# Two pooling groups per copy, pooling products later in the weave, and a weave paced by due times

## The chip, the cores and the metric

The kernel runs on one core of one Trainium2 chip. The metric is the device time of one execution in microseconds (us). Engines: PE is TensorE (matmul), DVE is VectorE, ACT is ScalarE, POOL is GpSimd, SP issues the weight transfers.

## The reference, cut to what matters

Two layers of a decoder trunk over 256 positions and 1024 channels, in float32. Each layer: half a SwiGLU, a mixer, half a SwiGLU, a gated embedding. The change lies in the mixer:

```
u = RMSNorm(h);  columns of u @ w_in go to three branches and their gates
A) sparse attention: indexer, top 64 keys of a query as a mask, softmax, values
B) pooling: for windows w = 2, 4, 8, 16, one group of 128 channels each:
       pooled = windowsum(x_g, w) / count - x_g ;  mixed = pooled @ w_pool[g] * scale
C) Mamba-2 SSD: conv, chunked scan in 2 chunks of 128, gated by silu(z), RMSNorm
h += W_out( sum_b sigmoid(gate_b) * Lift_b(branch_b) )
```

## The kernel before, in words

Everything is held with channels on partitions and the 256 positions in the free dimension. To keep float32 accuracy each operand is split into a high and a low part, and a product is three matmuls (`mm3`, L166 high-high, L167 low-high, L168 high-low). Weights stream in units of 128x1024: a DMA from SP into `raw`, a cast on ACT to `whi` (L140), a subtraction on DVE to `wlo` (L141). PSUM has two rings of four banks: `mm` for products with weights, `aux` for everything else.

In the mixer the work of the branches is written as Python generators, and `weave` takes steps from them in turn: always from the one whose share of steps done, `x[0] / x[3]`, is smallest. The number beside each generator is its count of steps. The scheduler of the tile framework then sets the order on each engine from its own estimate of times; instructions emitted with `keep` (and all in `mm`, L106, and `transpose`, L109) hold their order among themselves on PE.

There are two weaves a layer. The first has `choose` (indexer, top keys), `silus` (conv and gate inputs) and twelve steps of `gates`. The second has

- `states`: the SSD. Scans on DVE (L919), exponentials on ACT (L924), a product with the masked scores (L925), then `near` products on PE, added by L941; at the end of each half the carried state (L945, L952, L960, L962), the gate by silu(z) (L970), squares (L223, L225) and the split with the gain (L189, L190).
- `attend`: scores, `softmax` (L744 and L746 to L750), transposes of the probabilities (L109), copies (L761), values.
- `pools`: for two groups at a time the input projection into one bank of `mm`, then for each group `pool_group`: memset of a pad (L983), copy out of the bank (L984), one to four doubling adds (L988, L989), a correction (L993), the subtraction (L996), the split of the result (`split`, L185 and L186), and three matmuls with `w_pool`.
- `gate`: the rest of the gates' projections, plain `mm` work that fills PE.

`states` and `attend` are `apart`: when both have come to a step that yields a function, the functions are called one behind the other, so that the PE work with 64 rows or columns of both stands together. These are the common runs; there are four of them in a layer.

In `pool_group` a group's copy is emitted when its turn comes, so the second group's copy of a pair comes behind the first group's whole chain. The t1 buffers (six) hold the copy and all results of the chain. After the second weave come the lift products (in `mm` banks), the output projection and the next half.

Of the kernel before, what the change touches and what calls it, by code (L numbers as in the profile page):

```python
# [16 lines left out]
P = 128  # L17
D = 1024
S = 256
# [11 lines left out]

LINE = 128
WINDOWS = (2, 4, 8, 16)


CC = {}
# [28 lines left out]
class Builder:  # L65
    def __init__(self, ctx, tc, ins, out, order=None):
        self.tc = tc
        self.nc = tc.nc
        self.ins = ins
        self.out = out  # L70
        self.n = 0
        self.order, self.used, self.made = order, [], []
        self.todo = None
        self.gap = None

        def pool(name, bufs, **kw):
            return ctx.enter_context(tc.tile_pool(name=name, bufs=bufs, **kw))

        self.const = pool("const", 1)
        self.wp = pool("wp", 1)  # L80
        self.act = pool("act", 1)
        self.tmp = pool("tmp", 1)
        self.small = pool("small", 1)
        self.ps = pool("ps", 1, space=bass.MemoryType.PSUM)
        self.dram = pool("dram", 1, space=bass.MemoryType.DRAM)
# [328 lines left out]
    def in_steps(self, layer, i, u, ps):  # L414
        for j in range(2):
            w = self.unit(layer, U_IN + i + j, 1024)
            for k in range(KD):
                s = slice(k * P, (k + 1) * P)
                self.mm3(ps[:, j * S:(j + 1) * S], (w[0][:, s], w[1][:, s]),
                         (u[0][:, k], u[1][:, k]), k == 0, k == KD - 1)  # L420
                if k % 4 == 3:
                    yield

    def mix(self, layer, nxt):
# [63 lines left out]
        def choose():  # L488
            v4 = self.t([P, 4], tag="v4", bufs=1)
            nc.vector.tensor_scalar(v4[:, :2], ss[:, :2], 1.0 / 256, EPS, op0=OP.mult, op1=OP.add)  # L490
            nc.vector.tensor_scalar(v4[:, 2:], ss[:, 2:], 1.0 / 64, EPS, op0=OP.mult, op1=OP.add)
            rk = self.t([P, 4], tag="rk", bufs=1)
            self.rsqrt(rk, v4, 4)
            for h in range(2):
                nc.vector.tensor_scalar(cn[:, h], cn[:, h], rk[:, h:h + 1], None, op0=OP.mult)
                nc.vector.tensor_scalar(ki2[:, h], sm[:, h, None, 8:72].to_broadcast([P, 2, 64]),
                                        rk[:, 2 + h:3 + h], None, op0=OP.mult)
            yield
            yield
            yield  # L500
            pk = self.bank("aux")
            for h in range(2):
                self.transpose(pk[:, h * P:(h + 1) * P],
                                    ki2[:, h].rearrange("p a b -> p (a b)"), self.ident)
            self.split_scaled(ki[0], ki[1], pk[:, :S], self.col(layer, "idx_k_norm"))
            yield
            yield
            pc = self.bank("aux")
            for c in range(2):
                for h in range(2):  # L510
                    self.transpose(pc[:, c * S + h * P:c * S + (h + 1) * P],
                                        cn[:, h, c * P:(c + 1) * P], self.ident)
            for c in range(2):
                self.split_scaled(ct[:, 0, c], ct[:, 1, c], pc[:, c * S:(c + 1) * S],
                                  self.col(layer, "kv_norm", c))
            yield
            mb[0] = yield from self.indexer(layer, 0, sm, qi, ki, idx[:, 0])
            mb[1] = yield from self.indexer(layer, 1, sm, qi, ki, idx[:, 1])
# [32 lines left out]
        def some(n):  # L551
            for _ in range(n):
                next(gate)
                yield

        self.weave((choose(), 26), (silus(), 60), (some(12), 12))


        ya = self.a([P, 2, 4, S], FR, "a8", 2)
# [29 lines left out]
        def states():  # L589
            res["ssd"] = yield from self.ssd(layer, sm, xs, bc, cb, zs, big1[:, 16:22])  # L590

        def pools():
            wpl = self.unit(layer, U_POOL, 512)
            for i in range(0, 4, 2):
                ps = self.bank()
                yield from self.in_steps(layer, T_XP + i, u, ps)
                ps = ps.rearrange("p (a b) -> p a b", a=2)
                for j in range(2):
                    yield from self.pool_group(layer, i + j, ps[:, j], wpl, yp)

        with self.tc.issue_after(self.last.ins):
            self.weave((states(), 56), (attend(), 34), (pools(), 24), (gate, 43), apart=(0, 1))
        ysh, ysl, rs = res["ssd"]

        mh = self.a([P, 8, S], FR, "uh", 2)
# [39 lines left out]
    def weave(self, *gens, apart=()):  # L645

        left = [[0, i, g, n] for i, (g, n) in enumerate(gens)]  # L650
        apart, parked = set(apart), {}
        while left:
            x = min((x for x in left if x[1] not in parked), key=lambda x: (x[0] / x[3], x[1]))
            x[0] += 1
            call = next(x[2], x)
            if call is x:
                left.remove(x)
                apart.discard(x[1])
            elif call is not None:
                parked[x[1]] = call  # L660
            if parked and len(parked) == len(apart):
                for i in sorted(parked):
                    parked[i]()
                parked = {}

    def conv(self, layer, i, ps, xs, bc):
        nc = self.nc
# [63 lines left out]
    def softmax(self, h, two, mb, out):  # L731

        nc = self.nc
        nb = h + 1
        nk = nb * P
        per = 512 // nk
        prs = []
        for ps, _ in two:
            pr = self.t([P, per, nk])
            mx = self.t([P, per], tag="mx", bufs=2)  # L740
            sums = self.t([P, per], tag="sum", bufs=2)
            for j in range(per):
                x = mx[:, j:j + 1]
                nc.vector.tensor_tensor_reduce(pr[:, j], ps[:, j * nk:(j + 1) * nk], mb[:, :nk],  # L744
                                               1.0, 3.0e38, OP.add, OP.min, accum_out=x)
                self.last = nc.scalar.activation(pr[:, j], pr[:, j], AF.Exp, bias=x, scale=-1.0,  # L746
                                                 accum_out=sums[:, j:j + 1])
            nc.vector.reciprocal(sums, sums)
            for j in range(per):
                nc.scalar.mul(pr[:, j], pr[:, j], sums[:, j:j + 1])  # L750
            prs.append(pr)
            yield
        for _ in range(3):
            yield
        for (_, heads), pr in zip(two, prs):
            pt = self.bank("aux")
            for j in range(4):
                self.transpose(pt[:, j * P:(j + 1) * P],
                               pr[:, j // nb, (j % nb) * P:(j % nb + 1) * P], self.ident)
            th = self.t([P, 4, P])  # L760
            nc.scalar.copy(th, pt.rearrange("p (a b) -> p a b", a=4))  # L761
            out.append((heads, th))
            yield
# [211 lines left out]
        _, rs = self.rnorm(gap=2)  # L975
        return ysh, ysl, rs

    def pool_group(self, layer, g, ps, wpl, yp):
        nc = self.nc
        w = WINDOWS[g]  # L980
        pad = 16
        x = self.t([P, pad + S + 16], tag="t1")[:, :pad + S]
        nc.vector.memset(x[:, :pad], 0.0)  # L983
        nc.scalar.copy(x[:, pad:], ps)  # L984
        cur, have = x, 1
        while have < w:
            n = self.t([P, pad + S + 16], tag="t1")[:, :pad + S]
            nc.vector.tensor_copy(n[:, :have], cur[:, :have])  # L988
            nc.vector.tensor_tensor(n[:, have:], cur[:, have:], cur[:, :pad + S - have], op=OP.add)  # L989
            cur, have = n, 2 * have  # L990
        yield

        nc.vector.tensor_tensor(cur[:, pad:pad + 16], cur[:, pad:pad + 16],  # L993
                                self.col(layer, "pool_corr", g * 16, 16), op=OP.mult)
        y = self.t([P, S], tag="t1")
        nc.vector.scalar_tensor_tensor(y, cur[:, pad:], 1.0 / w, x[:, pad:],  # L996
                                       op0=OP.mult, op1=OP.subtract)
        yh = self.t([P, S], FR, tag="t1")
        yl = self.t([P, S], FR, tag="t1")
        self.split(yh, yl, y)  # L1000
        yield
        po = self.bank()
        s = slice(g * P, (g + 1) * P)
        self.mm3(po[:, :S], (wpl[0][:, s], wpl[1][:, s]), (yh, yl), True, True)
        self.split_scaled(yp[:, 0, g], yp[:, 1, g], po[:, :S], self.col(layer, "pool_scale", g))
# [211 lines left out]
```

## Time and profile before

| | us |
|---|---|
| median of 3 runs | 1339.59 (1339.23 to 1340.35) |
| the profiled execution | 1339.73 |
| its span, first to last instruction | 1338.0 |
| PE busy in the span | 1306.5 |
| DVE busy | 1044.9 |
| ACT busy | 741.8 |
| mean granted clock of PE | 0.993 |

Rows of the profile name an engine, the line of the kernel, the operation, output and inputs by the program's names, shapes and count. The first two numbers of a row of the timeline are its start in the span and how long it took; instructions of one engine overlap, so the next may start before one has ended. In brackets stands the idle time of the engine ahead of the row and what ended it. The second weave of layer 0 lies at about 295 to 395 us of the span, that of layer 1 at about 953 to 1052.

### The profile page before, as it was taken

The page shows a single profiled execution, that of the slowest core. Times are in us where ns is not written, and L with a number is a line of the kernel's source. Part 1 is how long each engine was busy: PE and PEld are TensorE (multiplying, and loading weights), DVE is VectorE, ACT ScalarE, POOL GpSimd, SP SyncE. Part 2 cuts the span into 40 slices and gives each one's busy share as a digit, 9 for nine tenths or more (in the row PEclk, how much of TensorE's full clock was granted, in tenths as well). Part 3 has the DMA queues.
Part 4 walks back from the last instruction along what each step waited for, and adds up shares of the span by engine and source line. Part 5 has one row for each costly group of instructions (what it writes and reads, how often), then busy time and mean ns, then how long its engine had stood idle before and what let it go on. Part 6 is the DMA issues. An engine that isn't in the chain of part 4 may idle for free.

```text
span 1338.0 us, 28291 instructions
## 1 busy us (share of the span) xinstructions
PE 1306.5 (98%) x11502; PEld 1296.9 (97%) x11502; DVE 1044.9 (78%) x1971; ACT 741.8 (55%) x1209; POOL 7.0 (1%) x17
## 2 busy tenths in 40 slices
PE   7999999999899999999999999999998999999997
PEld 7999999999899999999999999999988999999997
DVE  7877659987889787766887776799698888877666
ACT  6555446657664554544654454566486646554454
POOL 0000000000000000000000000000000000000000
PEclk9999999999899999999999999999999999999998
DMA  7666656566546666666656666566653566666661
GB/s 257 206 191 195 193 159 205 163 207 195 154 141 192 196 196 196 192 194 198 187 180 198 195 190 192 166 191 189 205 178 131 170 200 199 194 192 197 195 191 47
DMA packets 72386, 248.25 MB, mean 186 GB/s; under 512 B 7936, under 2 KB 10304, under 8 KB 72256
## 3 DMA queue, kind: packets, MB, share of 16 engines
q1 hardware_dynamic: 71392, 245.17, 59.6%
q8 instruction: 90, 1.47, 0.5%
q10 hardware_dynamic: 864, 1.28, 0.3%
q14 instruction: 40, 0.33, 0.1%
HBM read 245.33 MB, written 1.08 MB: 184 GB/s over the span
## 4 chain that ended last, share of the span: by engine, by line
PE 90%; DVE 5%; ACT 3%; issue 1%; DMA 1%; DVEq 0%; SPq 0%; ACTq 0%
PE mm L166 28%; PE mm L168 28%; PE mm L167 28%; PE aux L106 2%; DVE wlo L141 2%; ACT whi L140 1%; PE aux L109 1%; ACT t L746 1%; PE aux L167 1%; DVE ct L919 1%; PE aux L168 1%; PE aux L166 1%; DVE acc L225 0%; DMA h<-in_x_dram 0%; DMA raw<-in_w_dram 0%
## 5 line engine op out<-in xcount | busy, mean ns | idle before, releaser
L140 ACT CAST whi<-raw 128x1024 fp32r<-128x1024 f32 (+1 forms) x457 | 476.3, 1045 | 488.2 <-issue 230.3
L166 PE MATMUL mm<-uh,whi 128*128 128x256 f32 x2550 | 707.2, 279 | 6.9 <-ACT whi L160 6.8
L168 PE MATMUL mm<-uh,wlo 128*128 128x256 f32 x2560 | 708.7, 278 | 1.6 <-DVE wlo L141 1.6
L167 PE MATMUL mm<-ul,whi 128*128 128x256 f32 x2560 | 708.5, 277 | 0.1
L141 DVE TENSOR_TENSOR wlo<-raw,whi 128x1024 fp32r<-128x1024 f32 (+1 forms) x457 | 552.7, 1214 | 198.4 <-ACT whi L140 194.5
L166 PEld LDWEIGHTS mm<-uh,whi 128*128 128x128 f32 x2550 | 480.2, 189 | 8.4 <-ACT whi L160 6.8
L168 PEld LDWEIGHTS mm<-uh,wlo 128*128 128x128 f32 x2560 | 482.9, 189 | 2.6 <-DVE wlo L141 2.3
L167 PEld LDWEIGHTS mm<-ul,whi 128*128 128x128 f32 x2560 | 483.2, 189 | 0.4 <-DVE ul L190 0.4
L168 PE MATMUL mm<-gh,wlo 128*128 128x256 f32 x704 | 194.1, 276 | 0.0
L167 PE MATMUL mm<-gl,whi 128*128 128x256 f32 x704 | 194.1, 276 | 0.0
L166 PE MATMUL mm<-gh,whi 128*128 128x256 f32 x704 | 193.7, 276 | 0.0
L167 PEld LDWEIGHTS mm<-gl,whi 128*128 128x128 f32 x704 | 132.2, 188 | 0.0
L168 PEld LDWEIGHTS mm<-gh,wlo 128*128 128x128 f32 x704 | 132.2, 188 | 0.0
L166 PEld LDWEIGHTS mm<-gh,whi 128*128 128x128 f32 x704 | 131.9, 188 | 0.0
L166 PE MATMUL mm<-a,whi 128*128 128x256 f32 x256 | 70.9, 277 | 0.0
L168 PE MATMUL mm<-a,wlo 128*128 128x256 f32 x256 | 70.7, 276 | 0.0
L167 PE MATMUL mm<-a,whi 128*128 128x256 f32 x256 | 70.7, 276 | 0.0
L166 PEld LDWEIGHTS mm<-a,whi 128*128 128x128 f32 x256 | 48.1, 188 | 0.0
L167 PEld LDWEIGHTS mm<-a,whi 128*128 128x128 f32 x256 | 48.1, 188 | 0.0
L168 PEld LDWEIGHTS mm<-a,wlo 128*128 128x128 f32 x256 | 48.1, 188 | 0.0
L373 DVE TENSOR_TENSOR t<-mm,rs_r 128x256 f32<-128x256 f32 x88 | 37.2, 423 | 9.7 <-PE mm L168 0.6
L378 DVE SCALAR_TENSOR_TENSOR t<-t,t 128x256 f32<-128x256 f32 x88 | 37.4, 425 | 3.0
(221 smaller groups left out, 1102.8 us busy)
## 6 DMA issues: line engine op xcount, KB each, us to landing
raw<-in_w_dram SPq DMA_DIRECT2D x447, 512.0 KB, 4.2
gh<-rates SPq DMA_DIRECT2D x16, 256.0 KB, 3.6
raw<-in_w_dram SPq DMA_DIRECT2D x8, 352.0 KB, 3.1
raw<-in_w_dram SPq DMA_DIRECT2D x4, 256.0 KB, 3.9
gh<-rates SPq DMA_DIRECT2D x8, 128.0 KB, 3.6
h<-in_x_dram SPq DMA_DIRECT2D x2, 256.0 KB, 4.5
h<-in_x_dram SPq DMA_DIRECT2D x1, 512.0 KB, 6.2
t<-in_p_dram ACTq DMA_DIRECT2D x2, 256.0 KB, 5.8
```

The source lines that it names most:

```text
L106: self.tc.keep_in_program_order(self.nc.tensor.matmul(*args, **kw))
L109: self.tc.keep_in_program_order(self.nc.tensor.transpose(*args))
L140: nc.scalar.copy(hi[:, :n], raw[:, :n])
L141: ins = nc.vector.tensor_tensor(lo[:, :n], raw[:, :n], hi[:, :n].bitcast(F), op=OP.subtract)
L166: (self.mm if keep else mm)(ps, a[0], b[0], start=start, stop=False)
L167: mm(ps, a[0], b[1], start=False, stop=False)
L168: mm(ps, a[1], b[0], start=False, stop=stop)
L373: nc.vector.tensor_tensor(t, p1[0], r, op=OP.mult)
L378: nc.vector.scalar_tensor_tensor(g, th, 1.0, t, op0=OP.add, op1=OP.mult)
L746: self.last = nc.scalar.activation(pr[:, j], pr[:, j], AF.Exp, bias=x, scale=-1.0, accum_out=sums[:, j:j + 1])
L919: nc.vector.tensor_tensor_scan(m.rearrange("p a b -> p (a b)"), rate(g, h, q).rearrange("p a b -> p (a b)"), self.after.rearrange("p a b - ...
```

## The change: what it does

- `pools` copies both groups of a pair out of their bank into `px`, a buffer of its own (three rows of `big2`, two of which the indexer has used before), and takes one step of the weave before the first chain; `pool_group` reads from there.
- In `pool_group` two steps, not one, lie between the split of the operand and the three matmuls.
- `weave` keeps a due time for each generator and a place where it should end: each step moves the due time by the rest of the way over the rest of the steps, and a parked generator goes on from where the weave stands. The counts are set anew, with ends of 0.88 to 1.1.
- After a common run the next four half units of an input projection have their first matmul kept in order (`hold`).
- `softmax` takes 4 - h steps, not 3, ahead of its transposes (h is the half of the queries).

```
-        self.weave((choose(), 26), (silus(), 60), (some(12), 12))
+        self.weave((choose(), 28, 1.08), (silus(), 60, 1), (some(12), 12, 1))
...
 in pools():
             wpl = self.unit(layer, U_POOL, 512)
+            px = big2[:, 19:22].rearrange("p a b -> p (a b)").rearrange("p (a b) -> p a b", a=2)
+            px = px[:, :, :POOLPAD + S]
             for i in range(0, 4, 2):
                 ps = self.bank()
                 yield from self.in_steps(layer, T_XP + i, u, ps)
                 ps = ps.rearrange("p (a b) -> p a b", a=2)
                 for j in range(2):
-                    yield from self.pool_group(layer, i + j, ps[:, j], wpl, yp)
+                    nc.vector.memset(px[:, j, :POOLPAD], 0.0)
+                    nc.scalar.copy(px[:, j, POOLPAD:], ps[:, j])
+                yield
+                for j in range(2):
+                    yield from self.pool_group(layer, i + j, px[:, j], wpl, yp)
...
-            self.weave((states(), 56), (attend(), 34), (pools(), 24), (gate, 43), apart=(0, 1))
+            self.weave((states(), 55, 1), (attend(), 36, 1), (pools(), 22, 0.88), (gate, 48, 1.1),
+                       apart=(0, 1))
...
 in weave():
-            x = min((x for x in left if x[1] not in parked), key=lambda x: (x[0] / x[3], x[1]))
-            x[0] += 1
+            x = min((x for x in left if x[1] not in parked), key=lambda x: x[:2])
+            now = max(now, x[0])
             call = next(x[2], x)
+            x[0] += (x[4] - x[0]) / max(x[3], 1)
+            x[3] -= 1
...
                 for i in sorted(parked):
                     parked[i]()
+                for x in left:
+                    if x[1] in parked:
+                        x[0] = max(x[0], min(now, x[4]))
                 parked = {}
+                self.hold = 4
...
 in softmax():
-        for _ in range(3):
+        for _ in range(4 - h):
             yield
...
 in pool_group():
         self.split(yh, yl, y)
         yield
+        yield
         po = self.bank()
```

What the engines' orders show in layer 0 (numbers in names are running numbers of tiles; in the changed kernel L140 to L190 became L142 to L192, L919 is L939, L941 is L961, L983 is L606, L984 is L607, L989 is L1006, L993 is L1010, L996 is L1013).

DVE, the first group's chain, before:

```order
L989 TENSOR_TENSOR t_608_4222<-t_607_4219 128x271
L141 TENSOR_TENSOR wlo_4157<-raw_4155,whi_4156 128x1024
L993 TENSOR_TENSOR t_608_4222<-t_608_4222,cc_93 128x16
L941 TENSOR_TENSOR uh_2765<-uh_2765,aux_4246 128x4x128
L919 SCALAR_TENSOR_TENSOR ct_4378<-gh_2480,after 128x512 x2
L141 TENSOR_TENSOR wlo_4230<-raw_4228,whi_4229 128x1024
L996 SCALAR_TENSOR_TENSOR t_614_4248<-t_608_4222,t_607_4219 128x256
```

and now, where `gl` is the shared buffer `px`:

```order
L1006 TENSOR_TENSOR t_611_4244<-gl_2481 128x271
L143 TENSOR_TENSOR wlo_4157<-raw_4155,whi_4156 128x1024
L1010 TENSOR_TENSOR t_611_4244<-t_611_4244,cc_93 128x16
L606 MEMSET gl_2481 128x16
L1013 SCALAR_TENSOR_TENSOR t_621_4329<-t_611_4244,gl_2481 128x256
L143 TENSOR_TENSOR wlo_4228<-raw_4226,whi_4227 128x1024
L961 TENSOR_TENSOR uh_2765<-uh_2765,aux_4247 128x4x128
L939 SCALAR_TENSOR_TENSOR ct_4364<-gh_2480,after 128x512 x2
L188 TENSOR_TENSOR t_623_4332<-t_621_4329,t_622_4331 128x256
```

The subtraction has moved ahead of the add, the two scans and a weight split; the low half (L188) stands behind the scans.

ACT, the copies of the second pair, before: the third group's copy (of `mm_4447`), and eleven rows on the fourth group's.

```order
L984 COPY t_679_4684<-mm_4447 128x256
L189 ACTIVATE a_675_4659<-uh_2765,cc_93 128x256
L140 CAST whi_4632<-raw_4631 128x1024
L546 ACTIVATE gh_2480<-mm_4570 128x512
L189 ACTIVATE a_675_4659<-uh_2765,cc_93 128x256
L140 CAST whi_4705<-raw_4704 128x1024
L223 ACTIVATE t_683_4698<-uh_2765 128x256
L223 ACTIVATE t_688_4723<-uh_2765 128x256
L140 CAST whi_4753<-raw_4752 128x1024
L546 ACTIVATE gh_2480<-mm_4703 128x512
L185 CAST t_690_4731<-t_689_4729 128x256
L984 COPY t_697_4776<-mm_4447 128x256
```

and now:

```order
L225 ACTIVATE t_683_4727<-uh_2765 128x256
L191 ACTIVATE a_677_4701<-uh_2765,cc_93 128x256
L607 COPY gl_2481<-mm_4508 128x256 x2
L225 ACTIVATE t_684_4733<-uh_2765 128x256
L191 ACTIVATE a_677_4701<-uh_2765,cc_93 128x256
```

Both copies are one row, at the place of the first. DVE, what stands now behind the third group's subtraction and ahead of its low half (before, L186 followed the subtraction directly):

```order
L1013 SCALAR_TENSOR_TENSOR t_698_4825<-t_691_4779,gl_2481 128x256
L143 TENSOR_TENSOR wlo_4834<-raw_4832,whi_4833 128x1024
L961 TENSOR_TENSOR uh_2765<-uh_2765,aux_4831 128x4x128
L939 SCALAR_TENSOR_TENSOR ct_4895<-gh_2480,after 128x512 x2
L188 TENSOR_TENSOR t_700_4828<-t_698_4825,t_699_4827 128x256
```

PE, the third group's product, before:

```order
L167 MATMUL mm_4703<-ul_2732,whi_4553 128x256
L168 MATMUL mm_4703<-uh_2731,wlo_4554 128x256
L166 MATMUL mm_4770<-t_690_4731,whi_3786 128x256
L166 MATMUL mm_4830<-uh_2731,whi_4572 128x256
L167 MATMUL mm_4830<-ul_2732,whi_4572 128x256
```

and now:

```order
L169 MATMUL mm_4909<-ul_2732,whi_4644 128x256
L170 MATMUL mm_4909<-uh_2731,wlo_4645 128x256
L168 MATMUL mm_4928<-t_699_4827,whi_3786 128x256
L168 MATMUL mm_5012<-uh_2731,whi_4784 128x256
L169 MATMUL mm_5012<-ul_2732,whi_4784 128x256
```

Before, 120 matmuls with weights lie between the second common run and this product, all ahead of the third common run; now it stands behind the third common run, with 132 such matmuls and that run's products in between. The two matmuls with the low operands come 21 matmuls later before, 17 now.

More of the change, by code (lines that the diff above doesn't have):

```diff
@@ L33 @@
 WINDOWS = (2, 4, 8, 16)
+POOLPAD = 16
 CC = {}
@@ L74, in __init__ @@
         self.gap = None
+        self.hold = 0
         def pool(name, bufs, **kw):
@@ L418, in in_steps @@
                 s = slice(k * P, (k + 1) * P)
+                hold = k % 4 == 0 and self.hold > 0
+                self.hold -= hold
                 self.mm3(ps[:, j * S:(j + 1) * S], (w[0][:, s], w[1][:, s]),
-                         (u[0][:, k], u[1][:, k]), k == 0, k == KD - 1)
+                         (u[0][:, k], u[1][:, k]), k == 0, k == KD - 1, keep=hold)
                 if k % 4 == 3:
@@ L645, in weave @@
     def weave(self, *gens, apart=()):
-        left = [[0, i, g, n] for i, (g, n) in enumerate(gens)]
-        apart, parked = set(apart), {}
+        left = [[0.0, i, g, n, end] for i, (g, n, end) in enumerate(gens)]
+        apart, parked, now = set(apart), {}, 0.0
         while left:
-            x = min((x for x in left if x[1] not in parked), key=lambda x: (x[0] / x[3], x[1]))
-            x[0] += 1
+            x = min((x for x in left if x[1] not in parked), key=lambda x: x[:2])
+            now = max(now, x[0])
             call = next(x[2], x)
+            x[0] += (x[4] - x[0]) / max(x[3], 1)
+            x[3] -= 1
             if call is x:
@@ L976, in ssd, with pool_group @@
         return ysh, ysl, rs
-    def pool_group(self, layer, g, ps, wpl, yp):
+    def pool_group(self, layer, g, x, wpl, yp):
         nc = self.nc
         w = WINDOWS[g]
[L981 to L984, printed above, removed]
+        pad = POOLPAD
         cur, have = x, 1
```

## The prediction

> **What bounds the kernel now.** I read the page's busy table first, then the chain of waits of the matrix engine (PE), then a table of stretches, and last the rows of PE, DVE and ACT in the stretch that stands out. The page:
>
> ```profile
> span 1338.0 us, 28291 instructions
> PE 1306.5 (98%) x11502; PEld 1296.9 (97%) x11502; DVE 1044.9 (78%) x1971; ACT 741.8 (55%) x1209; POOL 7.0 (1%) x17
> ```
>
> PE is the bound: 31.5 us of the span are idle on it, and only those, and time at a lowered clock, can be won without taking work away. Who ended those waits (line waited for, total, times, longest):
>
> ```profile
> PE mm L166 <- ACT t L185: 10.9, 4, 4.8
> PE mm L166 <- ACT whi L160: 6.8, 1, 6.8
> PE aux L109 <- ACT t L750: 2.1, 2, 1.0
> PE mm L168 <- DVE wlo L141: 1.6, 3, 1.2
> ```
>
> The second row is the start of the kernel and the change does not touch it. The first is the pooling product waiting for its high operand (`split`, L185), twice a layer; the third is the softmax's transposes waiting for the scaled probabilities. Both lie in the second weave. Stretches there (us, busy PE, PEld, DVE, ACT, POOL with instruction counts, then granted clock):
>
> ```profile
> core 0: us, PE busy (x) PEld busy (x) DVE busy (x) ACT busy (x) POOL busy (x), PEclk, DMA share, GB/s
> 100.00:180.00 80.00, 80.00 (x708) 80.00 (x707) 54.23 (x79) 39.54 (x56) 0.00 (x0) 1.00 0.62 189
> 300.00:400.00 100.00, 93.51 (x838) 90.15 (x836) 82.32 (x170) 69.01 (x145) 0.00 (x0) 0.97 0.53 163
> 334.00:336.00 2.00, 1.36 (x5) 0.74 (x6) 1.78 (x3) 2.00 (x7) 0.00 (x0) 1.00 0.41 162
> 361.00:363.00 2.00, 1.41 (x6) 1.41 (x7) 1.46 (x7) 0.68 (x2) 0.00 (x0) 0.50 0.78 260
> 363.00:365.00 2.00, 2.00 (x12) 2.00 (x11) 1.73 (x7) 0.05 (x1) 0.00 (x0) 0.50 0.22 80
> 365.00:367.00 2.00, 2.00 (x11) 2.00 (x11) 0.42 (x1) 0.36 (x1) 0.00 (x0) 0.50 0.00 0
> 367.00:369.00 2.00, 2.00 (x16) 2.00 (x15) 0.48 (x1) 1.53 (x4) 0.00 (x0) 0.81 0.00 0
> 1020.00:1022.00 2.00, 2.00 (x10) 2.00 (x11) 1.86 (x10) 0.04 (x1) 0.00 (x0) 0.50 0.83 287
> 1022.00:1024.00 2.00, 2.00 (x15) 2.00 (x15) 1.40 (x5) 0.41 (x1) 0.00 (x0) 0.72 0.01 2
> ```
>
> From the first row a matmul costs 80/708 = 0.113 us. Behind the long wait PE runs at half clock: layer 0 loses 1.41x0.5 + 2x0.5 + 2x0.5 + 2x0.19 = 3.1 us, layer 1 loses 1.0 + 0.56 = 1.6 us. Behind a wait of 1 us the clock stays at 1.00 (334:336). The long wait itself, on PE and on ACT:
>
> ```profile
> 339.11 1.09 PE L106 MATMUL aux<-ct,ul 128*64 128x128 f32 x16
> 340.03 1.04 PE L106 MATMUL aux<-t,a 128*64 128x128 f32 x16
> 341.01 0.98 PE L106 MATMUL aux<-a,a 64*128 64x256 f32 x12
> 356.49 0.28 PE L168 MATMUL mm<-uh,wlo 128*128 128x256 f32 x1
> 361.59 0.58 PE L166 MATMUL mm<-t,whi 128*128 128x256 f32 x1 [4.83 <-ACT t L185]
> 361.97 0.41 PE L166 MATMUL mm<-uh,whi 128*128 128x256 f32 x1
> ```
>
> ```profile
> 352.85 0.35 ACT L984 COPY t<-mm 128x256 f32<-128x256 f32 x1
> 361.14 0.40 ACT L185 CAST t<-t 128x256 fp32r<-128x256 f32 x1 [2.70 <-DVE t L996]
> 361.45 0.37 ACT L984 COPY t<-mm 128x256 f32<-128x256 f32 x1
> ```
>
> The third group's values leave the bank at 352.85 and its operand is ready at 361.54. DVE never rests between: the window 353.3 to 361.2, grouped (times, mean ns):
>
> ```profile
> L141 DVE TENSOR_TENSOR wlo<-raw,whi 128x1024 fp32r<-128x1024 f32 x4 | 4.9, 1213 | 0.0
> L190 DVE SCALAR_TENSOR_TENSOR a<-uh,cc,a 128x256 fp32r<-128x256 f32 x4 | 1.9, 470 | 0.0
> L989 DVE TENSOR_TENSOR t<-t 128x271 f32<-128x271 f32 (+2 forms) x3 | 1.3, 426 | 0.0
> L225 DVE TENSOR_TENSOR acc<-acc,t 128x256 f32<-128x256 f32 x3 | 1.2, 413 | 0.0
> ```
>
> So the chain is mostly other work (weight splits, the SSD's output) standing ahead of three small adds. The fourth group's copy comes only at 361.45, and the first common work behind the wait, at 361.97, uses the bank that this copy empties (the ring has four). Two things hold PE there: the operand, and the bank.
>
> **The change, part by part.** Instruction counts of DVE, ACT and PE do not change; only places do. The copies cost the same 0.35 us each, now back to back, into a buffer of their own; the two memsets a pair are 0.07 us. These I cost at nothing.
>
> *First group (0.62 us a layer).* Before, between the correction (L993) and the subtraction (L996), DVE does:
>
> ```profile
> 322.21 0.67 DVE L941 TENSOR_TENSOR uh<-uh,aux 128x512 f32<-128x512 f32 x1
> 322.81 2.33 DVE L919 TENSOR_TENSOR_SCAN ct<-gh,after 128x512 f32<-128x512 f32 x2
> 325.06 1.19 DVE L141 TENSOR_TENSOR wlo<-raw,whi 128x1024 fp32r<-128x1024 f32 x1
> 326.17 0.41 DVE L996 SCALAR_TENSOR_TENSOR t<-t,t 128x256 f32<-128x256 f32 x1
> ```
>
> In the new order the subtraction stands ahead of the last split, the add and the two scans: 326.17 - 322.21 = 4.0 us earlier, against a product that PE reaches at the same place, 24 matmuls behind the first common run. The 0.62 us go. The low half stays behind the add and the scans and is now wanted at once: 0.61 + 2.25 + 0.43 = 3.3 us behind the near products, where PE has the scores and 24 matmuls, 1.5 + 2.7 = 4.2 us. Covered by 0.9 us, if DVE comes to the add on time.
>
> ```profile
> 321.95 1.56 PE L106 MATMUL aux<-a,a 64*128 64x128 f32 x24
> ```
>
> *Softmax transposes (1.04 us a layer).*
>
> ```profile
> 334.64 0.33 PE L109 MATMUL aux<-ident,t 128*128 128x128 f32 x1 [1.04 <-ACT t L750]
> ```
>
> Before, 75 matmuls lie between the scores and the second set of transposes, 8.5 us; in the new order 97, 11.0 us. Against that some pooling work, about 0.9 us, moves ahead of the softmax on DVE. 2.5 - 0.9 - 1.04 leaves 0.6 us to spare: the wait goes.
>
> *Third group (4.83 us a layer).* I count from the end of the SSD products of the second common run, 340.2. Before, PE reaches the product 16.6 us later (356.77) and the operand is there 21.3 us later (361.54). In the new order PE has from the same products to the product: 132 matmuls (14.9 us), the value products, scores and near products twice, one set of carried-state products and eight transposes, some 6.6 us by the rows above (1.04, 0.98, 0.92 and their like): 21.5 us of cover, 4.9 more. DVE has the same work up to the subtraction with one weight split fewer (five, not six): 21.3 - 1.1 = 20.2 us. The high operand is then 1.3 us early and the wait of 4.83 us goes. Its low half is not: behind the subtraction stand a split (1.13), an add (0.61), two scans (2.25) and then L188 (0.43), 4.4 us, while PE needs it at 0.44 + 1.3 + 17 matmuls and one (2.03) = 3.8 us. That leaves a new wait of 0.6 us a layer. If the high half is only just in time it is 1.9, if DVE comes to the run 0.6 us earlier it is nothing.
>
> *The bank.* Both copies now run 0.7 us together, ahead of the pooling chain, so the bank is free some 8 us earlier (353.5 for 361.8); no wait is left of it.
>
> *The clock.* The half-clock stretches came right behind the two waits of 4.83 us and nowhere else in the weave; with no wait over 2 us I take all of 3.1 + 1.6 = 4.7 us as gained. [...]
>
> *The tail.* From the last SSD near product PE has the values (1.0), the carried-state products (0.8), 48 gate matmuls and 24 of the lift, 9.9 us, before it needs the second normalised SSD half; DVE needs about 7.2 us for it (add 0.6, split 1.1, L186's kind 0.6, two of 0.6, four of 0.35, a split 1.1, 0.35, two of 0.4). Covered if DVE is not more than 2.7 us behind; I put 0.3 us a layer for that. In the first weave only one set of indexer products moves by 12 matmuls; PE has no idle time there, I take nothing.
>
> Sum: 10.9 + 2.1 + 4.7 = 17.7 us go, 2x(0.6 + 0.3) = 1.8 us come. The profiled execution took 1339.73 us (1338.0 of span and 1.7 around it), 0.14 above the median of the runs, 1339.59. 1339.59 - 15.9 = 1323.7 us. With nothing new it is 1321.9; with 1.9 us at the third group and 1 us more of tail a layer, 1327.7.
>
> **Rivals.**
> 1. *The wait moves onto DVE.* In 300:400 DVE is busy 82.3 of 100 us; with some 10 us less span it is 82.3/90 = 91%. If the low halves and the weight splits come late in turn, half of the 13.0 us stays, with half of the dips: 1339.6 - 6.5 - 2.35 = 1330.8. For it: DVE has no gap from 353 to 361. Against: it rests over 2 us right behind the wait, and a tenth of the time is left.
> 2. *The bank is the cause, and stays.* A buffer shared by both pairs must be read out before the second pair's copies; if they come as late as 361, the first gate product waits to 361.97 whatever the operands do, and only 0.62 and 1.04 us a layer go: 1336.3. [...] Against: in the new order the first pair's last subtraction stands ahead of the second common run, the copies behind it.
> 3. *The dips stay* (the clock follows something else in the weave): 1323.7 + 4.7 = 1328.4. Against: 1.00 at all waits of 1 us.
> 4. *Slower: the tail starves.* The new order leaves 48 gate matmuls behind the last run. If DVE is more than 2.7 us late there, PE stands at the first lift product of the SSD half, all matmuls queued behind it. It decides from (17.7 + 2.7)/2 - 2.35 = 7.8 us a layer with a dip; at 8.5 us: 1339.6 - 17.7 + 2x(8.5 + 2.35) = 1343.6. DVE would have to be 11 us behind; nothing shows that.
> 5. *Nothing changes*, because another order of the queues keeps the operand as late: 1339. The order rows speak against it.
>
> **How the numbers follow.** 0.2% (2.7 us) is about what a measurement of this kernel can tell from no change. Forecast 0.74 (1321.9 to 1327.7), rival 1 0.12, rival 2 0.03, rival 3 0.04, rival 4 0.04, rival 5 0.03. The range that leaves out at most 2 in 10 reaches from 1321.5 to 1331.0. Faster: 0.74 + 0.12 + 0.03 + 0.04 = 0.93; same 0.03; slower 0.04.
>
> **What would show it.** Right: no wait of PE over 2 us in either second weave, L187 gone from the top of PE's waits or below 2 us in all, no granted clock under 0.95 between 300 and 400 us, both L607 copies one behind the other, and a wait of PE for DVE L188 of about 0.6 us near the third product. Wrong: waits for L143 (DVE splits) or L192 of over 2 us a layer, a copy L607 later than the third product's place, or half clock without a wait ahead of it.

## The result, and the profile after

The changed kernel takes 1320.65 us (median of 4 runs, 1319.22 to 1320.67) against 1339.41 us for the kernel before in the same measurement: a ratio of 0.9856, with a 95% interval of 0.9839 to 0.9874. That is 3.05 us below the 1323.7 us of the forecast and 0.85 us below the low end of its range.

The page of the profiled execution (1320.67 us) and its list of PE's waits (line waited for, total, times, longest):

```profile
span 1319.0 us, 28294 instructions
PE 1300.4 (99%) x11502; PEld 1293.1 (98%) x11502; DVE 1041.0 (79%) x1971; ACT 740.8 (56%) x1209; POOL 7.0 (1%) x17
PE mm L168 <- ACT whi L162: 6.6, 1, 6.6
PE mm L170 <- DVE wlo L143: 1.7, 3, 1.2
PE aux L108 <- DVE acc L227: 1.0, 1, 1.0
PE aux L108 <- ACT t L225: 0.8, 1, 0.8
PE mm L168 <- ACT whi L142: 0.5, 1, 0.5
```

PE's idle time fell from 31.5 to 18.6 us. The waits for the pooling operand (10.9 us) and for the softmax (2.1 us) are gone from the list; what is left in it lies at the start of the kernel and at the norms. The stretches, with the columns of the table in the prediction:

```profile
300.00:400.00 100.00, 99.96 (x929) 97.68 (x928) 87.91 (x192) 72.11 (x148) 0.00 (x0) 1.00 0.54 169
361.00:363.00 2.00, 2.00 (x34) 1.80 (x33) 1.93 (x5) 2.00 (x3) 0.00 (x0) 1.00 0.43 72
14.00:16.00 2.00, 1.73 (x8) 1.73 (x9) 2.00 (x3) 1.32 (x2) 0.00 (x0) 0.62 0.42 76
16.00:18.00 2.00, 2.00 (x11) 2.00 (x11) 1.63 (x2) 0.24 (x1) 0.00 (x0) 0.53 0.95 313
```

In 300:400 PE is busy 99.96 us at full clock, where it was 93.51 at 0.97. The two lower rows are something else: this execution ran at half clock from 14.47 to 17.88 us, where the profiled execution of before stood at 1.00.

I measure the second weave from the first matmul of the SSD projection to the first lift product. In layer 0 these rows bound it:

```profile
296.27 0.28 PE L168 MATMUL aux<-ct,whi 128*128 128x256 f32 x1
385.44 0.28 PE L168 MATMUL mm<-a,whi 128*128 128x256 f32 x1
```

That is 89.17 us; before it was 395.06 - 295.40 = 99.66. Layer 1: 89.16, from 98.30. From one norm to the next, all other stretches of the two kernels agree within some 0.2 us, except the first weave of layer 0 (0.45 shorter) and the start (1.3 longer, by the half clock). So the gain is 10.49 + 9.14 us in the two stretches of the forecast.

The third group, where the long wait was: PE (the matmul with the high operand, the first with the low one and the row ahead of it), ACT and DVE; the last row of DVE begins the fourth group's chain.

```profile
365.49 0.28 PE L168 MATMUL mm<-t,whi 128*128 128x256 f32 x1
...
367.41 0.28 PE L169 MATMUL mm<-ul,whi 128*128 128x256 f32 x1
367.72 0.39 PE L169 MATMUL mm<-t,whi 128*128 128x256 f32 x1
```

```profile
356.41 0.61 ACT L607 COPY gl<-mm 128x256 f32<-128x256 f32 x2
363.46 0.41 ACT L187 CAST t<-t 128x256 fp32r<-128x256 f32 x1 [0.24 <-DVE t L1013]
```

```profile
362.95 0.42 DVE L1013 SCALAR_TENSOR_TENSOR t<-t,gl 128x256 f32<-128x256 f32 x1
363.29 1.22 DVE L143 TENSOR_TENSOR wlo<-raw,whi 128x1024 fp32r<-128x1024 f32 x1
364.42 0.68 DVE L961 TENSOR_TENSOR uh<-uh,aux 128x512 f32<-128x512 f32 x1
365.02 2.33 DVE L939 TENSOR_TENSOR_SCAN ct<-gh,after 128x512 f32<-128x512 f32 x2
367.27 0.40 DVE L188 TENSOR_TENSOR t<-t,t 128x256 fp32r<-128x256 f32 x1
367.65 0.43 DVE L1006 TENSOR_TENSOR t<-gl 128x271 f32<-128x271 f32 x1
```

The operand is ready at 363.87, in this execution 2.3 us later than before (361.54); 0.9 of that is the later start of the weave. PE comes to it at 365.49, 1.6 us after it. So the change did not make this operand earlier; it made PE come later. The first group's operand did come earlier: its cast ends 27.8 us behind the start of the weave, where it was 31.6.

### The profile page after: what moved, and what is told of

Read it like the earlier page. It is cut to its first block, busy times and chain, and to the rows that moved or that the text cites. A ratio compares the mean times of both kernels' runs of the same rounds, so it can differ in the third digit from the quotient of the medians.

```text
span 1319.0 us, 28294 instructions
## 1 busy us (share of the span) xinstructions
PE 1300.4 (99%) x11502; PEld 1293.1 (98%) x11502; DVE 1041.0 (79%) x1971; ACT 740.8 (56%) x1209; POOL 7.0 (1%) x17
## 3 DMA queue, kind: packets, MB, share of 16 engines
HBM read 245.33 MB, written 1.08 MB: 187 GB/s over the span
## 4 chain that ended last, share of the span: by engine, by line
PE 93%; DVE 3%; ACT 2%; issue 1%; DMA 0%; SPq 0%; DVEq 0%; ACTq 0%
PE mm L170 29%; PE mm L169 29%; PE mm L168 29%; PE aux L108 2%; DVE wlo L143 1%; PE aux L169 1%; PE aux L170 1%; PE aux L168 1%; PE aux L111 1%; ACT whi L142 1%; DVE ct L939 1%; DMA h<-in_x_dram 0%; PE mm L108 0%; ACT t L766 0%; DVE acc L227 0%
## 5 line engine op out<-in xcount | busy, mean ns | idle before, releaser
L142 ACT CAST whi<-raw 128x1024 fp32r<-128x1024 f32 (+1 forms) x457 | 476.3, 1045 | 488.4 <-issue 227.3
L168 PE MATMUL mm<-uh,whi 128*128 128x256 f32 x2518 | 696.2, 278 | 7.1 <-ACT whi L162 6.6
L168 PEld LDWEIGHTS mm<-uh,whi 128*128 128x128 f32 x2518 | 473.0, 188 | 7.8 <-ACT whi L162 6.6
```

The source lines that it names most:

```text
L142: nc.scalar.copy(hi[:, :n], raw[:, :n])
L168: (self.mm if keep else mm)(ps, a[0], b[0], start=start, stop=False)
```

## The experiments

All times stand beside runs of the kernel before on the same chip (medians 1338.9 to 1339.5 us). "Weave" is the length of the second weave, layer 0 and layer 1, in the profiled execution.

| kernel | median us | ratio, 95% interval | weave us | PE's waits in it, layer 0 |
|---|---|---|---|---|
| before | 1339.41 | 1 | 99.66, 98.30 | 0.62 + 1.04 + 4.83 |
| after | 1320.65 | 0.9856 (0.9839 to 0.9874) | 89.17, 89.16 | none listed |
| e_later | 1328.99 | 0.9921 (0.9906 to 0.9936) | 93.18, 93.24 | 0.63 + 1.04 + 1.14 |
| e_pair | 1346.77 | 1.0057 (1.0042 to 1.0072) | 101.76, 103.39 | 0.91 + 0.33 + 6.14 |
| e_pair_later | 1323.13 | 0.9883 (0.9867 to 0.9900) | 91.06, 91.15 | none |
| a_oneyield | 1342.44 | 1.0027 (1.0018 to 1.0036) | 100.77, 100.44 | 0.53 + 0.89 + 1.27 + 5.07 |
| a_nopair | 1343.75 | 1.0035 (1.0021 to 1.0049) | 100.62, 100.45 | 0.35 + 0.91 + 7.38 |
| a_nohold | 1322.62 | 0.9875 (0.9862 to 0.9889) | 90.10, 90.13 | none |
| e_hold4 | 1327.93 | 0.9913 (0.9900 to 0.9927) | 92.32, 92.33 | 0.60 + 1.42 |
| a_soft3 | 1321.21 | 0.9864 (0.9850 to 0.9877) | 90.03, 90.11 | 0.40 |
| a_fill | 1318.84 | 0.9845 (0.9832 to 0.9858) | 89.13, 89.12 | none |

**Operand or bank (e_later, e_pair).** The first adds the second `yield` to the kernel before, the second only the pair copies.

```
 e_later, in pool_group:            e_pair, in pools:
         yield                      +  for j in range(2):
+        yield                      +      nc.vector.memset(px[:, j, :POOLPAD], 0.0)
         po = self.bank()           +      nc.scalar.copy(px[:, j, POOLPAD:], ps[:, j])
                                    +  yield
                                       ...
```

> The kernel before with one edit: a second step of the weave between a pooling operand's split and its three products. Copies, weave and softmax stay as before. Theory (the wait of 4.83 us was the operand's, and the half clock behind it came from the wait): the product comes one turn later, so the waits for L185 (10.9 us) shrink to about 2 us a layer at the next product of the chain, the half clock (4.7 us) goes with them, the transposes stay: about 1329. Rival (the bank that the second group's copy holds is the cause, and the copies are as late as before): PE stands at the first gate product instead, 4 us or more a layer, with the half clock: 1336 to 1340.

> The kernel before with one edit: both groups of a pair are copied out of their bank ahead of the first chain, into the shared buffer, and one step of the weave follows the copies. The products stand one step behind their operand as before. Theory (operand): the product at the third group is still reached before its halves are ready, since the copies make no operand earlier on DVE; a wait of 4 to 7 us a layer stays, perhaps at the low half, with half clock behind it: 1333 to 1341. Rival (bank): the bank is free some 8 us earlier, the long wait and the half clock go: about 1324.

e_later, ACT's copies out of the bank (L984) and casts of the operand (L185) of the third and fourth group, and the two products:

```profile
356.02 0.36 ACT L984 COPY t<-mm 128x256 f32<-128x256 f32 x1
362.48 0.40 ACT L185 CAST t<-t 128x256 fp32r<-128x256 f32 x1
362.79 0.37 ACT L984 COPY t<-mm 128x256 f32<-128x256 f32 x1
374.36 0.40 ACT L185 CAST t<-t 128x256 fp32r<-128x256 f32 x1
```

```profile
365.75 0.39 PE L166 MATMUL mm<-t,whi 128*128 128x256 f32 x1
374.81 0.38 PE L166 MATMUL mm<-t,whi 128*128 128x256 f32 x1 [1.14 <-ACT t L185]
```

The fourth group's copy is as late as before (362.79), and no product waits for its bank: the wait of 4.83 us was the operand's. Whether the bank would have held PE at the old place, had the operand been in time there, no run shows. e_later met its theory (about 1329). In e_pair the fourth operand is cast at the same time as in e_later, but its product stands one step behind it:

```profile
374.34 0.39 ACT L186 CAST t<-t 128x256 fp32r<-128x256 f32 x1
374.78 0.58 PE L167 MATMUL mm<-t,whi 128*128 128x256 f32 x1 [6.14 <-ACT t L186]
```

So the pair copies by themselves make the kernel slower; 1346.8 us is over the range of either theory. I had the size of the wait (4 to 7 us) but not the place: the third product is covered, the fourth is not.

**Both pooling edits alone, and each undone (e_pair_later, a_oneyield, a_nopair).** The first is the kernel before with the two edits above. The others are the changed kernel with one of them undone (in a_nopair the step behind the copies goes with them):

```
 a_oneyield, in pool_group:         a_nopair, in pools and pool_group:
         yield                      -  for j in range(2):
                                       ...
-        yield                      -      nc.scalar.copy(px[:, j, POOLPAD:], ps[:, j])
         po = self.bank()           -  yield
                                    +  x = self.t([P, pad + S + 16], tag="t1")[:, :pad + S]
                                    +  nc.scalar.copy(x[:, pad:], ps)
                                       ...
```

> The kernel before with both edits to the pooling and nothing else: pair copies and two steps between operand and products, with the old weave (share of steps done), old counts, no held matmuls, three steps in the softmax. Theory (operand and bank together are the whole cause): no wait over 1 us in the second weaves, no half clock there, at most the transposes' wait stays (1.04 us a layer and about 0.9 us in which they run at the pace of ACT): 1320 to 1324. Rival (the even pace of the weave does it): a wait of 2 us or more a layer stays, 1328 or more.

> The changed kernel with one step, not two, between operand and products; pair copies and paced weave stay. Theory (operand): the products are reached before their halves; waits of 5 us or more a layer come back, half clock with them: 1335 to 1342. Rival (pace and copies are enough): 1321 to 1323.

> The changed kernel with each group's copy back behind the chain ahead of it, out of the bank, into a buffer of its own; two steps between operand and products, paced weave, held matmuls stay. Theory (the copies matter: a group's chain cannot begin before its copy, and the second copy of a pair stands behind the whole first chain, so the second group's operand is late and the bank stays taken): waits of 5 to 8 us a layer and half clock behind them, 1335 to 1345. Rival (moving the products was enough): 1321 to 1323.

The two edits alone bring 1323.13 us and no wait in the weaves; each one undone in the changed kernel loses all of the gain and more (a_oneyield 0.4 us over its range, with waits of 5.07 us for L187 in each layer). In a_nopair the fourth group's copy comes at 364.40, its operand is ready at 375.62, and PE waits 7.38 us:

```profile
364.40 0.37 ACT L998 COPY t<-mm 128x256 f32<-128x256 f32 x1
375.22 0.40 ACT L187 CAST t<-t 128x256 fp32r<-128x256 f32 x1 [0.71 <-DVE t L1010]
375.68 0.58 PE L168 MATMUL mm<-t,whi 128*128 128x256 f32 x1 [7.38 <-ACT t L187]
```

When is each operand ready, and when does PE come to its product? Both in us from the start of the weave in layer 0 (end of the cast; start of the matmul less the wait ahead of it):

| kernel | third group: operand, PE | fourth group: operand, PE |
|---|---|---|
| before | 66.1, 61.4 | 70.0, 73.8 |
| e_later | 66.4, 69.2 | 78.2, 77.2 |
| e_pair | 66.9, 68.6 | 78.9, 72.8 |
| e_pair_later | 69.7, 72.7 | 79.5, 80.6 |
| a_oneyield | 68.3, 63.3 | 72.4, 77.0 |
| a_nopair | 68.1, 68.8 | 80.9, 73.6 |
| after | 67.6, 69.2 | 77.9, 78.3 |

The long waits are the places where PE comes first. In no kernel is either operand earlier than before. With the old weave the pair copies leave the fourth operand no earlier either (e_pair 78.9, e_later 78.2), for its chain still stands behind the third group's, as in the changed kernel (DVE L1006 at 367.65, behind L1013 at 362.95); what they bring there is the step behind them, which moves the product. In the changed kernel, against a_nopair, the operand is 3.1 us earlier and PE 4.7 us later. A kernel with that step and without the pair copies was not run, so what the copies are worth by themselves stays open. In the old weave the second step alone brings 10 of the 16 us; in the paced weave neither edit does without the other.

**What the pace and the held matmuls add (a_nohold, e_hold4).** e_pair_later has no waits, yet its weaves are 1.9 us a layer longer than those of the changed kernel. In its second common run the transposes stand inside the products of the SSD:

```profile
334.49 0.27 PE L110 MATMUL aux<-ident,t 128*128 128x128 f32 x1
334.69 0.43 PE L107 MATMUL aux<-ct,ul 128*64 128x128 f32 x2
335.06 0.33 PE L110 MATMUL aux<-ident,t 128*128 128x128 f32 x1
...
336.30 0.33 PE L110 MATMUL aux<-ident,t 128*128 128x128 f32 x1
336.56 0.87 PE L107 MATMUL aux<-ct,ul 128*64 128x128 f32 x10
337.36 0.39 PE L169 MATMUL mm<-uh,wlo 128*128 128x256 f32 x1
```

From 334.49 to 337.36 are 2.87 us for 4 transposes and 16 products. Together and unbroken, four transposes take 0.36 us (354.68 to 355.04 in the changed kernel) and the 16 products of the first common run 1.02 (320.93 to 321.95 in the kernel before): 1.5 us are the price of going to and fro between 128*64 and 128*128 tiles, and the profile counts them as busy. The probabilities of these four were scaled by 334.35 (ACT), so they did not run at ACT's pace.

```
 a_nohold, in weave:                e_hold4 = e_pair_later, and in weave, softmax:
-                self.hold = 4      +                self.hold = 4
+                self.hold = 0      -        for _ in range(3):
                                    +        for _ in range(4 - h):
```

> The changed kernel without the held matmuls after a common run; everything else stays, and PE's order differs in one place a layer, where a pooling product stands inside the last common run and its two others inside the values behind it. Theory (each place where PE passes between 64-wide and 128-wide tiles costs about 0.1 us on either side, which the profile counts as busy): two places more, 0.25 us each, so 0.5 us a layer and 1 us in all: 1321 to 1322.5. Rival (a broken run costs nothing): within 0.5 us of 1320.65.

> The kernel before with both pooling edits, the held matmuls and the softmax's 4 - h steps; the old weave (share of steps done) and old counts stay. Common runs of layer 0 are whole but for one pooling product. Theory (the common runs broken up were the 2 us a layer that both pooling edits alone lacked; without the pace some transposes stand closer behind their scores): no broken-run loss, but a wait of 1 to 2 us a layer for the softmax: 1322 to 1326. Rival (the pace adds nothing of its own): 1319 to 1321.

One stretch each, PE from the last common run's first product to the end of its values, in a_nohold and then in the changed kernel (columns as above):

```profile
375.36:378.53 3.17, 3.17 (x37) 2.38 (x36) 3.17 (x8) 1.88 (x4) 0.00 (x0) 1.00 0.70 227
377.04:378.99 1.95, 1.95 (x33) 1.78 (x32) 1.95 (x6) 1.95 (x4) 0.00 (x0) 1.00 0.89 260
```

The first holds the three pooling matmuls as well, 0.34 us. 3.17 - 1.95 - 0.34 = 0.88 us for two interruptions, 0.44 each: nearly twice the 0.25 expected, and the whole of the 0.93 us that a layer is longer. The median is 2.0 us up, 0.1 over what the theory gave. e_hold4 came out 1.9 us above its upper end: of the 7.3 us over the changed kernel, 6.3 are the two weaves (waits of 1.42 and 0.60 us, and transposes at ACT's pace) and 1.0 a wait that nobody foresaw, 1.27 us for L227 at the norm ahead of layer 1's mixer.

e_hold4 differs from the changed kernel in the old weave and its counts alone, so pace and counts together are worth these 7.3 us there; which of the two does it was not tried. It is also 4.8 us slower than e_pair_later, which has neither the held matmuls nor the softmax's new steps and no wait for the softmax: in the old weave these two edits do harm.

**The softmax's steps (a_soft3).** The changed kernel with one line back:

```
-        for _ in range(4 - h):
+        for _ in range(3):
```

> The changed kernel with three steps of the softmax for both halves instead of 4 - h. In layer 0 two gate matmuls then stand between a common run and its values, and the transposes of the first half a matmul or so earlier. Theory (the transposes' wait went through the even pace, not through this edit): no wait of 1 us, one more place where 64-wide and 128-wide tiles meet, some 0.45 us a layer: 1321 to 1322.5. Rival (the edit of the softmax took the wait away): 1.04 us of wait and 0.86 us of transposes at the pace of ACT a layer come back: 1324 to 1325.

The transposes' wait does not come back; 0.9 us a layer do, a wait of 0.40 us and an interrupted run. The median is only 0.6 us up; the profiled execution kept the full clock at the start, where that of the changed kernel lost it. The edit takes no large wait away.

**The clock, by itself (a_waits).** Behind the end of the changed kernel stand bursts of 100 matmuls, each with a wait of a chosen length ahead of it; there is one execution of it. In short:

```
for k in (0, 2, 4, 6, 8, 1, 3, 5, 7, 10, 2, 0, 3, 1, 4, 6):
    100 x self.mm(ps, w, x);  t = copy(ps);  k x (t -= o);  x = cast(t)
```

> The changed kernel with a measurement behind its end: 17 bursts of 100 matmuls (128x128 by 256, all in one order) with a copy, k subtractions of 128x256 on DVE (k from 0 to 10) and a cast between one burst and the next, so that PE waits by steps of about 0.4 us, from about 1.2 to about 5.5 us. A burst at full clock takes 11.4 us. Theory (the clock halves for whole windows): behind short waits a burst takes 11.4 us, from some wait between 1.3 and 4.8 us on it takes 1.7 or 3.4 us more, and nothing between these. Rival (the loss grows with the wait): bursts lengthen step by step. The kernel's own part ends at about 1319 us of the span.

Six of the bursts: start, length, and in brackets the wait ahead.

```profile
1494.16 12.14 PE L108 MATMUL aux<-t,t 128*128 128x256 f32 x100 [1.87 <-ACT t L1143]
1521.71 12.25 PE L108 MATMUL aux<-t,t 128*128 128x256 f32 x100 [2.28 <-ACT t L1143]
1423.86 13.75 PE L108 MATMUL aux<-t,t 128*128 128x256 f32 x100 [2.33 <-ACT t L1143]
1358.95 13.74 PE L108 MATMUL aux<-t,t 128*128 128x256 f32 x100 [2.74 <-ACT t L1143]
1394.56 13.48 PE L108 MATMUL aux<-t,t 128*128 128x256 f32 x100 [4.58 <-ACT t L1143]
1477.96 14.33 PE L108 MATMUL aux<-t,t 128*128 128x256 f32 x100 [5.55 <-ACT t L1143]
```

All seven waits up to 2.28 us cost nothing, the eight from 2.33 to 4.58 us cost 1.3 to 1.6 us over 12.2 (not 11.4, as expected of a burst), and 5.55 us cost 2.1. It is a step, as the theory says, and the amounts lie below its 1.7 and 3.4, the halves of the 3.4 and 6.8 us for which the clock of before stood at 0.50. In the burst from 1358.95 the half clock ran from 1360.06 to 1363.47, all of it in the work, and cost 1.5 us: 0.44 us a microsecond, not 0.5. Only behind 4.58 and 5.55 us does part of the half clock lie in the wait.

The length of the wait is not what decides, though. In before, in after and here the clock changes only at instants that are whole multiples of 3.413 us apart (before: 360.92 and 1019.69, 193 of them; after: 14.47 and 1311.54, 380; here 1360.06, 1377.12, 1424.91 and the others). In stretches between such instants, the wait of 2.33 us and then that of 2.28:

```profile
1421.50:1424.91 3.41, 1.08 (x9) 1.05 (x9) 1.27 (x3) 0.78 (x2) 0.00 (x0) 1.00 0.02 5
1424.91:1428.33 3.42, 3.42 (x19) 3.42 (x18) 0.00 (x0) 0.00 (x0) 0.00 (x0) 0.50 0.00 0
1517.07:1520.49 3.42, 2.37 (x20) 2.16 (x19) 0.57 (x2) 0.37 (x1) 0.00 (x0) 1.00 0.00 0
1520.49:1523.90 3.41, 2.19 (x18) 2.19 (x19) 0.70 (x2) 0.40 (x1) 0.00 (x0) 1.00 0.00 0
1523.90:1527.31 3.41, 3.41 (x30) 3.41 (x30) 0.00 (x0) 0.00 (x0) 0.00 (x0) 1.00 0.02 5
```

The first wait lies in one stretch, PE is busy 1.08 us of it, and the next stretch has half clock. The second is cut in two by a boundary, 1.05 and 1.22 us, and the clock stays. In the seven bursts without loss no stretch holds more than 1.36 us of idle time; in the nine with loss one holds 2.29 us or more. A single wait of 1.4 to 2.2 us inside one stretch was not tried.

**The start (a_fill).** 14 matmuls whose result nobody reads go ahead of the second weight unit, where PE waits 0.51 and 1.24 us for weights.

```
+                    if first and f == 0 and j == 1:
+                        pf = self.bank("aux")
+                        for _ in range(14):
+                            self.mm(pf[:, :S], u[0][:, 7, :P], u[0][:, 7], start=True, stop=True)
                     ...
-                             keep=f == 1 and j == 0)
+                             keep=f == 1 and j == 0 or first and f == 0 and j == 1)
```

> The changed kernel with 14 matmuls more (128x128 by 256, result unused) ahead of the second weight unit of the kernel's first half, where PE waits 0.51 and 1.24 us for weights and some runs fall to half clock for 1.7 us at 14 to 18 us of the span. Theory (the half clock there comes from the idle time of these waits, and varies from run to run): with the wait filled the clock stays and the 1.7 us are never lost; all runs near the lowest of the changed kernel, 1319 to 1319.8. Rival (the half clock is the warming up of a cold start, at a fixed time): as the changed kernel or 1.5 us longer by the matmuls: 1320.5 to 1322.

```profile
12.00:14.00 2.00, 2.00 (x18) 2.00 (x18) 1.90 (x4) 2.00 (x3) 0.00 (x0) 1.00 0.34 139
14.00:16.00 2.00, 2.00 (x19) 2.00 (x18) 2.00 (x2) 1.21 (x2) 0.00 (x0) 1.00 0.56 129
16.00:18.00 2.00, 2.00 (x20) 2.00 (x20) 1.30 (x2) 0.46 (x1) 0.00 (x0) 1.00 0.85 299
```

The clock stays at 1.00, and all five runs lie between 1318.79 and 1319.14 us: 1.8 us less than the changed kernel, in part under the theory's 1319 even, and the fastest kernel of all. Of the other eleven profiled executions three (after, e_later, e_pair) fell back to half clock there, with 1.60 to 1.74 us of idle time in the stretch ahead; seven, with at most 1.57 us in any stretch once they had the full clock, did not, and e_hold4 began only 12 matmuls from 16 to 18 us, the pace of half clock, and 19 from 18 to 20.

## Why the prediction was right, and where not

*Right.* The waits go: 0.62 + 1.04 + 4.83 us a layer, as written. The third operand was to be ready 20.2 us after the SSD products of the second common run and PE to come 21.5 us after them; from 343.5 it was 363.87 - 343.5 = 20.4 and 365.49 - 343.5 = 22.0. The half clock followed the waits and went with them; by half-microsecond stretches it ran from 360.9 to 367.7 and from 1019.7 to 1023.1, behind waits that ended at 361.59 and 1019.81, which at half the time is (367.7 - 361.6)/2 = 3.1 and 1.6 us, the two terms of the sum. Half is a little too much: at half clock matmuls begin 0.213 us apart there (361.97, 362.19 and 362.40 before), at full clock 0.115, so 46% of the time is lost, 2.8 and 1.5 us. The 0.4 us too much hid, by luck, a part of the two errors below. The half clock lasted 3.4 us in layer 1 and twice that in layer 0: there 0.67 us of the wait lie behind the fall of the clock at 360.92, in layer 1 only 0.12 us behind that at 1019.69.

*Rivals.* Rival 2 (the bank) falls by e_later, rival 3 (the dips stay) by the clock of 1.00. Rival 1 (the wait moves to DVE) did not happen: DVE rose to 87.9 us of 100, not 91, and no product waits for it by more than 0.3 us. No wait stands in the tail (rival 4).

*Wrong: two terms of the sum.* The waits went by the mechanism that was written; the sizes of these two did not hold.

1. The softmax transposes were priced at their listed wait, 1.04 us. Beside it they ran at ACT's pace, each behind its own scaling (L750). Before (PE, then ACT), and four such transposes after:

```profile
334.64 1.21 PE L109 MATMUL aux<-ident,t 128*128 128x128 f32 x4 [1.04 <-ACT t L750]
334.20 1.27 ACT L750 ACTIVATE t<-t,sum 128x128 f32<-128x128 f32 x4
354.68 0.60 PE L111 MATMUL aux<-ident,t 128*128 128x128 f32 x4
```

From start to the next instruction the four took 335.81 - 334.64 = 1.17 us, freely 355.04 - 354.68 = 0.36; 0.8 us a layer were lost in a group that the page counts as busy. Moved behind their data they lose neither: 1.6 us more gain in all. e_hold4, where they stand too early again, has the group back at 1.21 us.

2. The new waits, 0.6 us at the third low half and 0.3 us in the tail a layer, were 0.20 us in layer 0 (367.72, where 367.41 + 0.11 was due), 0.28 in layer 1, and nothing in the tail. The place was right: L188 stands behind the split, the add and the scans, 4.3 us for the 4.4 forecast. Its cover was longer, since PE came to the high half 1.6 us behind the operand, not 1.3. 1.3 us of the 1.8 did not come.

The sum with these sizes, and 0.4 us less for the half clock: 15.9 + 1.6 + 1.3 - 0.4 = 18.4. The half clock at the start takes 1.3 of it in the profiled execution, the first weave of layer 0 gives 0.45, which makes 17.6; measured were 1339.73 - 1320.67 = 19.1. The cause of the 1.5 us between, some 0.6 of it in each second weave, stays open.

The range's low end stood 0.4 us under the case with nothing new (1321.9), so it held no room for a term that was missing, only for terms that fail.

## What to carry to other kernels

When an operand is late, ask first whether its product can come later; here one line that moved the products brought 10 of the 19 us (e_later), and no long wait was left only when the next product of the chain was covered too. A row of several instructions behind a wait may be paced by their producer: compare its time with the same group elsewhere before pricing only the idle time in brackets (here 1.17 us for four transposes, 0.36 when nothing held them). Keep small-tile work in unbroken runs; here an interruption cost 0.44 us (a_nohold) without any wait to show for it.

## What the runs showed of the hardware

- In the bursts of a_waits the clock followed PE's idle time inside fixed stretches of 3.413 us: up to 1.36 us left it alone, 2.29 us and more halved it for the next stretch. So a wait of 2.28 us across a boundary cost nothing and one of 2.33 us inside a stretch cost 1.5 us.
- Several short waits in one stretch did it too: 0.51 and 1.24 us at the start (after, 11.06 to 14.47), and in e_pair, layer 1, 0.91 and 0.33 us between 993.43 and 996.85, where four transposes at ACT's pace also stand; behind them the clock was halved to 1000.26, and the weave came out 1.6 us longer than in layer 0. In layer 0 a boundary at 334.66 parts the same two waits, and the clock stayed. At the end of before 1.21 us of idle time were enough (1326.90 to 1330.31, beside transposes and products of one column): the clock stood at 0.50 from there on.
- The half clock behind a wait lasted one or two of these stretches (1424.91 to 1428.32 in a_waits, 360.92 to 367.74 in before) and could begin after work had resumed: behind the wait of 2.33 us PE started at 1423.86, and the clock fell at 1424.91.
- An interruption of a run of 64-wide products by 128-wide matmuls cost 0.44 us (a_nohold).
